# Program order on three engines, and weights halved two dense tiles ahead, in a two-layer decoder step

## Chip, core and metric

The kernel runs on one core of one Trainium2 chip. The metric is the device time of one execution in microseconds (us).

## What is computed

Two layers of a causal decoder for a prompt of 1024 tokens and a group of 8 sample tokens, which together are 1032 columns of a transposed stream `x` (8 blocks of 128 channels).

- Layer 0: RMS norm, one projection into an HGRN2 group and an attention group, an output projection `w_out0`, residual. Then RMS norm and ConvFFN, residual.
- Layer 1: RMS norm, Conformer convolution (GLU from `w_pw1`, depthwise convolution of width 31, LayerNorm over channels, swish, `w_pw2`), residual. Then RMS norm and ConvFFN, residual.
- A final RMS norm.

ConvFFN, with 22 blocks of 128 channels:

```python
g, u = split(h @ w_in)
gc = dwconv3(concat(hist, g))
out = (gelu(gc) * u) @ w_out
```

## The kernel before

**Halved numbers.** Every dense product is made from two parts of each operand: a high part, which ScalarE rounds (`ACT.copy`), and a low part, the difference, which VectorE (or GpSimd) takes. `split` (L102) does it, and `dense2` (L1030) issues three matmuls for each of 8 blocks of the contraction: high by high, high by low, low by high. For weights, `prep` (L106) loads a block of 512 KB into one of two raw buffers (tag `wr`) and `split_halves` (L122) makes two high and two low halves of 128x512. Tags `wh` and `wl` have four buffers each, that is two blocks. Blocks of `w_ffn_out` go through the same two raw buffers, and GpSimd takes their low halves (`oh`, `ol`, six buffers each).

**Tiles.** The columns are worked in two halves: half 0 has 512 columns (24 matmuls a dense tile), half 1 has 520, as two pieces of 260 (48 matmuls). In `mlp` (L1144) `f_in(f)` makes one FFN tile: a dense tile for the gate; ScalarE evacuates it into `gx`, takes the first step of the filter of width 3 and later the GELU; VectorE takes two filter steps; a dense tile for `u`; VectorE's product; the split of that into `ah` and `al`; the output block's load and halves. Behind every second `f_in`, `f_out` makes the output products of the two FFN tiles before (48 matmuls in half 0, 96 in half 1) and VectorE adds them to `x`. Two FFN tiles with one such `f_out` are called a pair here. `f_out_last` (L1228) does the last pair of all, and `finish` (L1389) makes one final tile of 128 tokens: transposes, sum of squares, a reciprocal root by 11 VectorE instructions on one column (`rsqrt_column`), product, store.

**Side work.** Norms and the convolution are generators in the queue `side`. `tick()` (L1119) grants them `rate[0]` units of cost, and each piece yields what it costs. `conv` (L1297) works channel block by channel block: 21 taps on VectorE, accumulated in PSUM (L1318, L1320), and 10 that ScalarE scales (L1304, L1308) and GpSimd adds (L1309); 21 taps with what is beside them cost 15.5 units. `rms_norm` (L1086) and `norm_ln` (L1348) make sums of squares, a mean over channels by a matmul (L1057), and scaled, split outputs. The rates are 2.6, 2.2 in the second projection, and 3.0 in the MLP that carries the second convolution.

**Order of stages from 670 us on:** `w_out0` for half 1; MLP of layer 0, half 0; the same, half 1, five FFN tiles; GLU of half 0 (8 channel blocks), with the first convolution on the side from here; the rest of that MLP; `w_pw2` for half 0; GLU of half 1; MLP of layer 1, half 0, with the second convolution, and within it, after 19 FFN tiles, `w_pw2` for half 1; MLP of layer 1, half 1.

**Order of instructions.** The planner orders each engine's instructions ahead of time, by what it reckons to be ready. From L1415 on TensorE alone is taken out of that and runs in the order of the program:

```python
order.enter_context(tc.manual_schedule(engines={mybir.EngineType.PE}))
```

Of the kernel before, what the change touches and what calls it, by code (L numbers as in the profile page):

```python
# [24 lines left out]
KD = 8  # L25
# [8 lines left out]
def tile_hybrid_step(  # L34
# [76 lines left out]
    class Halves:  # L111


        def __init__(self, pool, tag, bufs):
            self.t = [pool.tile([P, 4, P], F32R, name=tag, tag=tag, bufs=bufs) for _ in range(2)]
# [12 lines left out]
    def wcols(w, c0):  # L128
        return w[:, c0:c0 + P].rearrange("(k p) m -> p k m", p=P)
# [863 lines left out]
    LOW[:] = None, None  # L993
    Y1 = mixed(1)
# [113 lines left out]
    def project(W, h, xt, bias=None):  # L1108
        for m in range(KD):
            w = prep(wcols(W, m * P))  # L1110
            ps = mm2()
            dense2(ps, w, xt, h)
            add_res(m, h, ps, None if bias is None else pv[:, bias + m:bias + m + 1])
            tick()
# [4 lines left out]
    def tick():  # L1119
        side.step(rate[0])  # L1120
# [23 lines left out]
    def mlp(l, h, xt, finish=None):  # L1144
# [14 lines left out]
        def f_in(f):  # L1159
            fc = slice(f * P, (f + 1) * P)  # L1160
            wd = [wfd[:, l, t, f:f + 1] for t in range(3)]
            w = prep(wcols(w_ffn_in[l], f * P))
            ps = mm2()
            dense2(ps, w, xt, h)
# [19 lines left out]
            for t in (1, 2):  # L1184
                DVE.scalar_tensor_tensor(out=ga, in0=gx[:, t:t + m], scalar=wd[t], in1=ga,  # L1185
                                         op0=ALU.mult, op1=ALU.add)
            actf(ga, ga, AF.Gelu)
            tick()
            w = prep(wcols(w_ffn_in[l], NF * P + f * P))
            ps = mm2()  # L1190
            dense2(ps, w, xt, h)
# [8 lines left out]
            wr = wp.tile([P, KD, P], F32, name="wor", tag="wr")  # L1200
            SP.dma_start(wr.rearrange("p k m -> p (k m)"), w_ffn_out[l][fc, :])
            oh, ol = split_halves(wr, fp, "oh", "ol", 6, POOL)
            acts[f] = (ah, al, oh, ol)
            tick()

        def f_out(fs):
            js = [(acts[f][a], acts[f][b]) for f in fs for a, b in ((2, 0), (2, 1), (3, 0))]
            if h == 0:
                for m in range(0, KD, 2):
# [5 lines left out]
                    if m % 4:  # L1215
                        tick()
            else:
                for m in range(KD):
# [6 lines left out]
                    if m % 4 == 3:  # L1225
                        tick()

        def f_out_last(fs):  # L1228

            js = [(acts[f][a], acts[f][b]) for f in fs for a, b in ((2, 0), (2, 1), (3, 0))]  # L1230
            for q in range(2):
# [9 lines left out]
                for t in ((4, 5), (6, 7, 8))[q]:  # L1241
                    for _ in finish(t):
                        pass
# [29 lines left out]
    def glu(k, h, xt):  # L1273
        n = HN[h]
        wa = prep(wcols(w_pw1[0], k * P))
        wg = prep(wcols(w_pw1[0], T + k * P))
        if h == 0:
            pa = pg = mm2()
        else:
            pa, pg = mm2(), mm2()  # L1280
        dense2(pg, wg, xt, h, 1)
        tick()
        dense2(pa, wa, xt, h, 0)
        sg = scratch("ga", 2)[:, :n]
# [214 lines left out]
```

## Time and profile before

| | us |
|---|---|
| median of 3 runs | 2626.59 (2624.08 to 2627.39) |
| the profiled execution | 2624.44 |
| its span, first to last instruction | 2622.7 |

The profile is one execution. Its times are microseconds from the span's start. PE is TensorE's matmuls, PEld its weight loads, DVE VectorE, ACT ScalarE, POOL GpSimd, SP the engine that issues most loads. A row `A <-B` after a bracket or bar says how long the engine was idle before the instruction and what ended that. Matmuls overlap, so the duration of one is more than the spacing of two; the spacing is the stretch divided by the number of them. The mean granted clock of TensorE over the span is 0.981 of full speed.

### The profile page before, as it was taken

Reading aid. Unit: us, or ns where it says so; the run is one execution under the profiler, and the core shown is the slowest. Engines: PE = TensorE matmul, PEld = TensorE weight load, DVE = VectorE, ACT = ScalarE, POOL = GpSimd, SP = SyncE. Lnnn points to the kernel's source line nnn. Section 1 sums busy time; section 2 is a strip of 40 time slices with the busy share of each in tenths; the row PEclk is TensorE's granted clock in tenths of the full one; section 3 lists DMA queues with packets and bytes.
Section 4 is the critical chain, followed back from the end, with each engine's and each line's share of the span. In section 5 each row is a group of like instructions: output and inputs, shape, how many; then the busy total and the mean of one; then the engine's idle time right before and its main releaser. Section 6 shows DMA issues by size and latency. Waiting matters only on the chain.

```text
span 2622.7 us, 40721 instructions
## 1 busy us (share of the span) xinstructions
PE 2484.9 (95%) x15819; PEld 2229.3 (85%) x15819; DVE 1789.2 (68%) x3138; ACT 1229.2 (47%) x2124; POOL 737.1 (28%) x718
## 2 busy tenths in 40 slices
PE   7999998988999999999998999998999998999997
PEld 7888887876978888797998998997777787999997
DVE  7777767776565555479878866859998665654455
ACT  5566645654453333355344455555454542433332
POOL 2111245244211111116354330056663101111110
PEclk9999999999999999999999999999999999999999
DMA  6222244336233333232322322333323322333321
GB/s 200 69 66 65 58 113 141 97 101 187 89 111 98 97 93 100 72 101 81 90 80 74 97 82 65 90 91 97 88 81 97 105 79 79 118 98 90 89 82 57
DMA packets 319908, 247.06 MB, mean 94 GB/s; under 512 B 12055, under 2 KB 292039, under 8 KB 319683
## 3 DMA queue, kind: packets, MB, share of 16 engines
q1 hardware_dynamic: 308899, 213.09, 27.7%
q0 software_dynamic: 10816, 31.38, 4.0%
q8 instruction: 124, 2.03, 0.3%
q14 instruction: 69, 0.57, 0.1%
HBM read 226.82 MB, written 18.73 MB: 94 GB/s over the span
## 4 chain that ended last, share of the span: by engine, by line
PE 36%; DVE 9%; DMA 3%; issue 2%; POOL 2%; ACT 2%; SPq 0%; POOLq 0%; DVEq 0%; ACTq 0%
PE mm L1040 18%; PE mm L1222 9%; PE mm L1037 6%; PE mm L1213 2%; DVE wl L104 2%; DVE dacc L1320 2%; DMA wr<-in_w_ffn_in 2%; DVE ga L1185 1%; DMA wor<-in_w_ffn_out 1%; POOL ol L104 1%; DVE x L1214 1%; ACT wh L103 1%; POOL dp L1309 0%; DVE ga L1195 0%; DVE al L104 0%
## 5 line engine op out<-in xcount | busy, mean ns | idle before, releaser
L103 ACT CAST wh<-wr 128x512 fp32r<-128x512 f32 x536 | 327.0, 617 | 719.7 <-PE mm L1040 280.7
L104 DVE TENSOR_TENSOR wl<-wr,wh 128x512 fp32r<-128x512 f32 x512 | 398.7, 785 | 359.3 <-ACT wh L103 357.5
L1040 PE MATMUL mm<-xn,wh 128*128 128x260 f32 x3840 | 623.2, 285 | 3.1 <-DVE U L1402 2.3
L1037 PE MATMUL mm<-xn,wh 128*128 128x512 f32 x1792 | 558.6, 393 | 2.0 <-ACT wh L103 1.9
L1040 PEld LDWEIGHTS mm<-xn,wh 128*128 128x128 f32 x3840 | 529.9, 189 | 6.3 <-issue 2.9
L104 POOL TENSOR_TENSOR ol<-wor,oh 128x512 fp32r<-128x512 f32 x176 | 245.2, 1412 | 755.0 <-ACT oh L103 408.1
L1037 PEld LDWEIGHTS mm<-xn,wh 128*128 128x128 f32 x1792 | 339.3, 190 | 73.9 <-ACT wh L103 3.1
L1040 PE MATMUL mm<-xn,wl 128*128 128x260 f32 x1920 | 388.3, 284 | 2.6 <-DVE wl L104 2.6
L141 PE MATMUL mm<-xn,wh 128*128 128x260 f32 (+2 forms) x1584 | 385.0, 330 | 0.5 <-ACT qraw L309 0.5
L1037 PE MATMUL mm<-xn,wl 128*128 128x512 f32 x896 | 352.8, 394 | 10.1 <-DVE wl L104 10.0
L1040 PEld LDWEIGHTS mm<-xn,wl 128*128 128x128 f32 x1920 | 297.5, 190 | 2.8 <-DVE wl L104 2.8
L141 PEld LDWEIGHTS mm<-xn,wh 128*128 128x128 f32 x1584 | 267.5, 192 | 27.7 <-issue 8.3
L141 PE MATMUL mm<-xn,wl 128*128 128x260 f32 (+2 forms) x792 | 258.3, 326 | 0.2 <-DVE wl L104 0.2
L1320 DVE SCALAR_TENSOR_TENSOR dacc<-U,wdw,dacc 128x512 f32<-128x512 f32 x304 | 228.1, 750 | 4.7
L1309 POOL TENSOR_TENSOR dp<-dp,s 128x512 f32<-128x512 f32 x144 | 198.7, 1380 | 89.5 <-ACT s L1308 83.7
L1037 PEld LDWEIGHTS mm<-xn,wl 128*128 128x128 f32 x896 | 169.5, 189 | 50.9 <-DVE wl L104 15.3
L1185 DVE SCALAR_TENSOR_TENSOR ga<-gx,wfd,ga 128x544 f32<-128x544 f32 (+1 forms) x176 | 143.0, 813 | 45.6 <-ACT ga L1183 43.4
L1102 DVE TENSOR_TENSOR x<-x,mm 128x520 f32<-128x520 f32 x176 | 121.4, 692 | 63.2 <-PE mm L1222 55.7
L141 PEld LDWEIGHTS mm<-xn,wl 128*128 128x128 f32 x792 | 151.7, 192 | 12.3 <-issue 2.4
L103 ACT CAST oh<-wor 128x512 fp32r<-128x512 f32 x176 | 104.9, 618 | 119.6 <-DMA wor<-in_w_ffn_out 51.7
L1222 PE MATMUL mm<-ah,oh 128*128 128x260 f32 x672 | 140.3, 291 | 19.7 <-DVE ga L1197 10.0
L1213 PE MATMUL mm<-ah,oh 128*128 128x512 f32 x352 | 142.7, 405 | 14.1 <-DVE ga L1195 9.0
(380 smaller groups left out, 4003.4 us busy)
## 6 DMA issues: line engine op xcount, KB each, us to landing
wr<-in_w_ffn_in SPq DMA_DIRECT2D x176, 512.0 KB
wor<-in_w_ffn_out SPq DMA_DIRECT2D x88, 512.0 KB
wr<-in_w_pw SPq DMA_DIRECT2D x48, 512.0 KB
wr<-in_w_in SPq DMA_DIRECT2D x28, 512.0 KB
wr<-in_w_out SPq DMA_DIRECT2D x16, 512.0 KB
xt<-in_x_prompt SPq DMA_DIRECT2D x8, 512.0 KB
xtd<-xs POOLq DMA_DIRECT2D x8, 512.0 KB, 5.2
cb<-cumd SPq DMA_DIRECT2D x8, 512.0 KB
```

The costliest lines, as they stand in the source:

```text
L103: ACT.copy(h, raw)
L104: (eng or DVE).tensor_tensor(out=l, in0=raw, in1=h.bitcast(F32), op=ALU.subtract)
L141: PE.matmul(ps, a[k], b[:, k, :], start=k == order[0] and j == 0, stop=k == order[-1] and j == 2)
L1037: PE.matmul(ps[:, i], a[k], xt[:, r, k], **f)
L1040: PE.matmul(ps[:, q, 0:260], a[k], xt[:, r, k, q * 260:q * 260 + 260], **f)
L1102: DVE.tensor_tensor(out=ways(x[:, m, sl], h), in0=ways(x[:, m, sl], h), in1=outs(ps, h), op=ALU.add)
L1185: DVE.scalar_tensor_tensor(out=ga, in0=gx[:, t:t + m], scalar=wd[t], in1=ga, op0=ALU.mult, op1=ALU.add)
L1213: PE.matmul(ps[:, q], o[m + q], a, start=i == 0, stop=i == len(js) - 1)
L1214: DVE.tensor_tensor(out=x[:, m:m + 2, LO], in0=x[:, m:m + 2, LO], in1=ps, op=ALU.add)
L1222: PE.matmul(ps[:, q, 0:260], o[m], a[:, q * 260:q * 260 + 260], start=i == 0, stop=i == len(js) - 1)
L1309: POOL.tensor_tensor(out=dps[k], in0=dps[k], in1=q, op=ALU.add)
L1320: ins = DVE.scalar_tensor_tensor(out=o, in0=src, scalar=w, in1=accs[k], op0=ALU.mult, op1=ALU.add)
```

## The change

- From L1415 on TensorE, VectorE and ScalarE run in the order of the program; GpSimd and the load queue stay with the planner.
- A table `uses` lists every weight block from the second half of `w_out0` on, in the order of use. `Feed` loads from it through the same two raw buffers and halves dense blocks two dense tiles ahead. Four halves are made before the first tile. After that each dense tile takes one block with `feed.next()`, and two calls of `feed.halve("W")` behind its matmuls make one half each: the first right behind the matmuls, the second behind the evacuation or the residual add. `feed.block()` halves an output block at the end of its FFN tile, with GpSimd taking the low halves as before. A raw buffer's next load is issued when its second half has been made.
- `tick` takes a weight: 0.85 twice in an FFN tile; in `f_out` 0.7 for each of four steps, where it was a whole tick for two.
- The GLU's two tiles take a PSUM tile each, the gate's sigmoid comes before the second tile.
- The projection inside the MLP of layer 1 comes after 18 FFN tiles, not 19.
- In `f_out_last`, final tiles 4 and 5 come behind blocks of the second half, and tiles 6, 7 and 8 after all of them; `finish` takes its reciprocal root for these three from ScalarE's logarithm and exponential and one Newton step of four VectorE instructions.

```diff
+    AT = 18
+
+    def ffn(l, f0=0, f1=NF):
+        for f in range(f0, f1):
+            yield "W", wcols(w_ffn_in[l], f * P)
+            yield "W", wcols(w_ffn_in[l], NF * P + f * P)
+            yield "O", w_ffn_out[l][f * P:(f + 1) * P, :]
+
+    def columns(w):
+        for m in range(KD):
+            yield "W", wcols(w, m * P)
...
+    def glus():
+        for k in range(KD):
+            yield "W", wcols(w_pw1[0], T + k * P)
+            yield "W", wcols(w_pw1[0], k * P)
+
+    uses = [*columns(w_out0[0]), *ffn(0), *ffn(0, 0, 5), *glus(), *ffn(0, 5), *columns(w_pw2[0]),
+            *glus(), *ffn(1, 0, AT), *columns(w_pw2[0]), *ffn(1, AT), *ffn(1)]
+
+    class Feed:
+
+
+        def __init__(self):
+            ws = [u for u in uses if u[0] == "W"]
+            self.seq, n = ws[:2], 2
+            for u in uses:
+                if u[0] == "O":
+                    self.seq.append(u)
+                elif n < len(ws):
+                    self.seq.append(ws[n])
+                    n += 1
+            self.raw, self.q, self.i, self.half, self.cur = {}, [], 0, 0, None
+            self.last = 1 + max(i for i, u in enumerate(self.seq) if u[0] == "W")
+            self.load(0)
+            self.load(1)
+
+        def load(self, i):
+            if i < len(self.seq):
+                kind, ap = self.seq[i]
+                wr = self.raw[i] = wp.tile([P, KD, P], F32, name="wr", tag="wr")
+                SP.dma_start(wr if kind == "W" else wr.rearrange("p k m -> p (k m)"), ap)
+
+        def halve(self, kind):
+
+            if kind == "W" and self.i >= self.last:
+                return
+            assert self.seq[self.i][0] == kind
+            pool, th, tl, bufs = (wp, "wh", "wl", 4) if kind == "W" else (fp, "oh", "ol", 6)
+            if self.half == 0:
+                self.cur = Halves(), Halves()
+                if kind == "W":
+                    self.q.append(self.cur)
+            i = self.half
+            h, l = (pool.tile([P, 4, P], F32R, name=t, tag=t, bufs=bufs) for t in (th, tl))
+            split(self.raw[self.i][:, 4 * i:4 * i + 4], h, l, POOL if kind == "O" else None)
+            self.cur[0].t.append(h)
+            self.cur[1].t.append(l)
+            if i:
+                del self.raw[self.i]
+                self.load(self.i + 2)
+                self.i += 1
+            self.half = 1 - i
+
+        def block(self):
+            self.halve("O")
+            self.halve("O")
+            return self.cur
+
+        def next(self):
+            return self.q.pop(0)
+
+    feed = Feed()
+    for _ in range(4):
+        feed.halve("W")
...
-    def project(W, h, xt, bias=None):
+    def project(h, xt, bias=None):
         for m in range(KD):
-            w = prep(wcols(W, m * P))
             ps = mm2()
-            dense2(ps, w, xt, h)
+            dense2(ps, feed.next(), xt, h)
+            feed.halve("W")
             add_res(m, h, ps, None if bias is None else pv[:, bias + m:bias + m + 1])
+            feed.halve("W")
             tick()
 
     RATE, PROJ, CONV = 2.6, 2.2, 3.0
     rate = [RATE]
 
-    def tick():
-        side.step(rate[0])
+    def tick(w=1.0):
+        side.step(rate[0] * w)
...
             wd = [wfd[:, l, t, f:f + 1] for t in range(3)]
-            w = prep(wcols(w_ffn_in[l], f * P))
             ps = mm2()
-            dense2(ps, w, xt, h)
+            dense2(ps, feed.next(), xt, h)
+            feed.halve("W")
...
                                          op0=ALU.mult, op1=ALU.add)
+            feed.halve("W")
             actf(ga, ga, AF.Gelu)
-            tick()
-            w = prep(wcols(w_ffn_in[l], NF * P + f * P))
+            tick(0.85)
             ps = mm2()
-            dense2(ps, w, xt, h)
+            dense2(ps, feed.next(), xt, h)
+            feed.halve("W")
...
             split(t, ah, al)
-            wr = wp.tile([P, KD, P], F32, name="wor", tag="wr")
-            SP.dma_start(wr.rearrange("p k m -> p (k m)"), w_ffn_out[l][fc, :])
-            oh, ol = split_halves(wr, fp, "oh", "ol", 6, POOL)
+            feed.halve("W")
+            oh, ol = feed.block()
             acts[f] = (ah, al, oh, ol)
-            tick()
+            tick(0.85)
 
...
-                    if m % 4:
-                        tick()
+                    tick(0.7)
...
-                    if m % 4 == 3:
-                        tick()
+                    if m % 2:
+                        tick(0.7)
...
-                for t in ((4, 5), (6, 7, 8))[q]:
-                    for _ in finish(t):
-                        pass
+                    if q and m in (2, 4):
+                        run(finish(3 + m // 2))
+            for t in (6, 7, 8):
+                run(finish(t))
...
-        wa = prep(wcols(w_pw1[0], k * P))
-        wg = prep(wcols(w_pw1[0], T + k * P))
-        if h == 0:
-            pa = pg = mm2()
-        else:
-            pa, pg = mm2(), mm2()
-        dense2(pg, wg, xt, h, 1)
+        pg = mm2()
+        dense2(pg, feed.next(), xt, h)
+        feed.halve("W")
+        sg = scratch("ga", 2)[:, :n]
+        actf(ways(sg, h), outs(pg, h), AF.Sigmoid, bias=pv[:, PV["bpw1"] + 8 + k:PV["bpw1"] + 9 + k])
+        feed.halve("W")
         tick()
-        dense2(pa, wa, xt, h, 0)
-        sg = scratch("ga", 2)[:, :n]
-        actf(ways(sg, h), outs(pg, h, 1), AF.Sigmoid, bias=pv[:, PV["bpw1"] + 8 + k:PV["bpw1"] + 9 + k])
+        pa = mm2()
+        dense2(pa, feed.next(), xt, h)
+        feed.halve("W")
         DVE.scalar_tensor_tensor(out=ways(U[:, k, 30:30 + n], h), in0=outs(pa, h),
                                  scalar=pv[:, PV["bpw1"] + k:PV["bpw1"] + k + 1],
                                  in1=ways(sg, h), op0=ALU.add, op1=ALU.mult)
+        feed.halve("W")
...
+        if t > 5:
+
+            actf(y[:n], ss[:n], AF.Ln, bias=eps_c[:n], scale=1.0 / 1024.0)
+            actf(y[:n], y[:n], AF.Exp, scale=-0.5)
+            DVE.tensor_scalar(out=ss[:n], in0=ss[:n], scalar1=1.0 / 1024.0, scalar2=None,
+                              op0=ALU.mult)
+            newton(y[:n], a[:n], ss[:n], EPS)
...
-    order.enter_context(tc.manual_schedule(engines={mybir.EngineType.PE}))
+    order.enter_context(tc.manual_schedule(engines={mybir.EngineType.PE, mybir.EngineType.Activation,
+                                                  mybir.EngineType.DVE}))
...
-    projected, idle = False, 0
-    for f in range(NF):
-        run(m, 1)
-        idle += not side.q
-        if not projected and (idle == 2 or f == NF - 4):
-            side.drain()
-            project(w_pw2[0], 1, ZB[0], PV["bpw2"])
-            side.add(rms_norm(1, PV["ffn"] + 8, B))
-            projected = True
+    run(m, AT)
+    side.drain()
+    project(1, ZB[0], PV["bpw2"])
+    side.add(rms_norm(1, PV["ffn"] + 8, B))
```

## Rows read from the trace of the kernel before

**Rows 1.** The page, busy time: engine, us, share of the span, instructions.

```profile
PE 2484.9 (95%) x15819; PEld 2229.3 (85%) x15819; DVE 1789.2 (68%) x3138; ACT 1229.2 (47%) x2124; POOL 737.1 (28%) x718
```

**Rows 2.** Busy time by stage: PE, PEld, DVE, ACT, POOL; then PE clock, DMA share, GB/s.

```profile
1094.00:1170.00 76.00, 73.08 (x584) 72.40 (x584) 48.65 (x87) 36.98 (x61) 12.30 (x10) 0.97 0.32 92
...
1170.00:1267.30 97.30, 91.59 (x387) 72.31 (x386) 85.74 (x112) 52.09 (x84) 57.10 (x41) 0.98 0.30 88
...
1267.30:1608.20 340.90, 323.87 (x2616) 321.26 (x2615) 262.96 (x434) 160.24 (x257) 127.41 (x100) 0.97 0.28 81
...
1751.00:2081.70 330.70, 308.48 (x1307) 248.18 (x1308) 294.52 (x376) 175.73 (x296) 172.51 (x140) 0.97 0.31 91
...
2127.80:2203.30 75.50, 70.90 (x294) 56.58 (x292) 47.25 (x63) 29.27 (x48) 11.25 (x9) 0.95 0.26 77
...
2250.40:2587.80 337.40, 337.22 (x2808) 336.96 (x2806) 167.49 (x324) 117.27 (x193) 57.26 (x48) 1.00 0.30 87
...
2587.80:2622.70 34.90, 19.13 (x138) 17.38 (x136) 20.82 (x76) 6.55 (x12) 1.01 (x2) 0.83 0.17 62
```

**Rows 3.** The same columns by pair of FFN tiles, or for several pairs together.

```profile
832.30:1029.70 197.40, 197.40 (x866) 162.29 (x865) 102.26 (x132) 71.79 (x120) 34.45 (x36) 1.00 0.33 96
...
1302.00:1337.00 35.00, 35.00 (x294) 35.00 (x293) 16.13 (x30) 16.15 (x27) 14.21 (x12) 1.00 0.29 86
...
1337.00:1496.80 159.80, 145.51 (x1162) 144.76 (x1161) 143.21 (x227) 70.73 (x117) 80.90 (x61) 0.96 0.28 83
...
1751.00:1789.60 38.60, 35.26 (x146) 28.21 (x147) 32.96 (x40) 25.00 (x42) 28.90 (x24) 0.96 0.37 105
...
1789.60:1970.90 181.30, 170.09 (x722) 136.46 (x721) 175.81 (x226) 90.33 (x155) 111.54 (x90) 0.98 0.29 86
...
1970.90:2005.60 34.70, 33.42 (x146) 26.93 (x145) 27.96 (x37) 12.97 (x24) 9.14 (x8) 1.00 0.36 102
...
2005.60:2048.80 43.20, 36.81 (x154) 29.54 (x153) 31.27 (x41) 24.54 (x41) 17.07 (x14) 0.92 0.29 86
```

**Rows 4.** Timeline of ScalarE, VectorE and TensorE near 1335 us.

```profile
1332.99 1.34 ACT L1308 ACTIVATE s<-U,wdw 128x512 f32<-128x512 f32 x2 [0.65 <-POOL dp L1309]
...
1334.23 0.61 ACT L103 CAST wh<-wr 128x512 fp32r<-128x512 f32 x1
...
1334.87 1.38 DVE L104 TENSOR_TENSOR wl<-wr,wh 128x512 fp32r<-128x512 f32 x1 [6.39 <-ACT wh L103]
...
1346.03 0.77 PE L1222 MATMUL mm<-ah,oh 128*128 128x260 f32 x2 [6.09 <-DVE ga L1197]
```

**Rows 5.** Groups on VectorE, 1770 to 1980 us; the last row 1350 to 1500.

```profile
L1320 DVE SCALAR_TENSOR_TENSOR dacc<-U,wdw,dacc 128x512 f32<-128x512 f32 x121 | 90.7, 750 | 1.8
...
L104 DVE TENSOR_TENSOR wl<-wr,wh 128x512 fp32r<-128x512 f32 x48 | 45.8, 954 | 3.8 <-ACT wh L103 3.7
...
L1185 DVE SCALAR_TENSOR_TENSOR ga<-gx,wfd,ga 128x512 f32<-128x512 f32 x24 | 23.5, 980 | 0.0
...
L104 DVE TENSOR_TENSOR al<-ga,ah 128x512 fp32r<-128x512 f32 x13 | 14.6, 1122 | 0.3 <-ACT ah L103 0.3
...
L1320 DVE SCALAR_TENSOR_TENSOR dacc<-U,wdw,dacc 128x512 f32<-128x512 f32 x73 | 54.7, 749 | 0.8
```

**Rows 6.** Busy time of line 1320 alone in the GLU of half 0.

```profile
1170.00:1267.30 97.30, 46.85 (x63) 0.98 0.30 88
```

**Rows 7.** Timeline of VectorE in the last tile.

```profile
2589.51 0.70 DVE L104 TENSOR_TENSOR al<-ga,ah 128x520 fp32r<-128x520 f32 x1 [0.74 <-ACT ah L103]
```

**Rows 8.** The chain that ended last, near 1372 us: start, us, what.

```profile
1372.17 3.99 DMA wr<-in_w_ffn_in
```

**Rows 9.** Groups on VectorE, 850 to 1000 us.

```profile
L104 DVE TENSOR_TENSOR wl<-wr,wh 128x512 fp32r<-128x512 f32 x36 | 25.0, 706 | 40.2 <-ACT wh L103 40.1
```

**Rows 10.** Line 1094: ns least/median/most, first and last start.

```profile
L1094 DVE SCALAR_TENSOR_TENSOR s<-x,pv,hy x48: 741/749/1798, 687.9 to 2163.0; 128x512 f32<-128x512 f32 x24, 128x520 f32<-128x520 f32 x24
```

**Rows 11.** Timeline of TensorE in the last output blocks.

```profile
2602.07 0.39 PE L1236 MATMUL mm<-ah,oh 128*128 128x260 f32 x1 [1.14 <-DVE x L1239]
```

More of the change, by code (lines that the diff above doesn't have):

```diff
@@ L111, in tile_hybrid_step, with __init__ @@
     class Halves:
-        def __init__(self, pool, tag, bufs):
-            self.t = [pool.tile([P, 4, P], F32R, name=tag, tag=tag, bufs=bufs) for _ in range(2)]
+        def __init__(self, pool=None, tag=None, bufs=0):
+            self.t = [] if pool is None else [pool.tile([P, 4, P], F32R, name=tag, tag=tag, bufs=bufs) for _ in range(2)]
         def __getitem__(self, k):
@@ L1159, in f_in @@
         def f_in(f):
-            fc = slice(f * P, (f + 1) * P)
             wd = [wfd[:, l, t, f:f + 1] for t in range(3)]
-            w = prep(wcols(w_ffn_in[l], f * P))
             ps = mm2()
-            dense2(ps, w, xt, h)
+            dense2(ps, feed.next(), xt, h)
+            feed.halve("W")
             gx = fp.tile([P, 546], F32, name="gx", tag="gx", bufs=2)
@@ L1397, in finish @@
         ACT.activation(row(1)[:n], ps[:n], AF.Square, accum_out=ss[:n])
-        DVE.tensor_scalar(out=ss[:n], in0=ss[:n], scalar1=1.0 / 1024.0, scalar2=EPS,
-                          op0=ALU.mult, op1=ALU.add)
-        rsqrt_column(y[:n], a[:n], ss[:n])
+        if t > 5:
[4 more added lines that the diff above has]
+            newton(y[:n], a[:n], ss[:n], EPS)
+        else:
+            DVE.tensor_scalar(out=ss[:n], in0=ss[:n], scalar1=1.0 / 1024.0, scalar2=EPS,
+                              op0=ALU.mult, op1=ALU.add)
+            rsqrt_column(y[:n], a[:n], ss[:n])
         yo = row(2 + t % 2)
@@ L1414, in tile_hybrid_step @@
     order = ExitStack()
-    order.enter_context(tc.manual_schedule(engines={mybir.EngineType.PE}))
+    order.enter_context(tc.manual_schedule(engines={mybir.EngineType.PE, mybir.EngineType.Activation,
+                                                  mybir.EngineType.DVE}))
     A, B, ZA, ZB = [], [], [], []
     side.add(rms_norm(0, PV["ffn"], A))
-    project(w_out0[0], 1, Y1)
+    project(1, Y1)
     side.drain()
@@ L1434, in tile_hybrid_step @@
     side.add(rms_norm(1, PV["mix"] + 8, B))
-    project(w_pw2[0], 0, ZA[0], PV["bpw2"])
+    project(0, ZA[0], PV["bpw2"])
     side.drain()
```

## Prediction

> **What bounds the kernel now.** I read the busy shares first: TensorE is busy 95% of the span [rows 1], so only its idle time is to be had, and the windows by stage say where that lies [rows 2]. In the plain stretch of the last MLP (2250.4 to 2587.8) TensorE waits for nothing: 2808 records in 337.4 us, 0.120 us each. In a quiet stretch with 512 columns 866 stand in 197.4 us, 0.228 each [rows 3]. These two spacings times a stage's matmuls give what it needs. A pair of FFN tiles with its output blocks has 144 matmuls in half 0, 32.9 us (six pairs in the 197.4), and 288 and a few transposes in half 1, 34.8 (the undisturbed pair from 1302 has 35.0 [rows 3]). The reader is to see in the stages:
> - the GLU of half 0: 384 matmuls, 87.4 us, took 97.3: 10 lost;
> - the MLP of layer 0, half 1, before it: 576 matmuls and some others, 71, took 76.0: 5 lost;
> - the same MLP after the GLU: 2592 and some others, 316, took 340.9: 25 lost;
> - the MLP of layer 1 up to the projection: 1296 and some means, 299, took 330.7: 32 lost;
> - the rest of that MLP: 288, 67, took 75.5: 8 lost;
> - the end: 34.9 us for some 16 us of matmuls and transposes.
>
> The two large losses carry the depthwise convolution, and there VectorE is nearly the bound: in five pairs of half 0 it is busy 175.8 of 181.3 us, in four of half 1 143.2 of 159.8 [rows 3]. The first is a full engine. The second is not: VectorE waits 6.39 us for a weight half, because ScalarE's order has convolution taps ahead of it that are held by GpSimd, and then TensorE stands 6.09 us [rows 4]. So the loss is partly VectorE's amount of work and partly the planner's order.
>
> **Taps in a pair.** A tap takes 0.75 us. In half 0 121 of the common form (19 of every 21) stand in 210 us, 23 in a pair of 36.3; in half 1 73 in 150 us, 21.5 in a pair of 40 [rows 5]. After the change the ticks are 4 x 0.85 + 4 x 0.7 = 6.2 a pair instead of 6; with 15.5 units for 21 taps that is 25.2 taps at 3.0 units (half 0) and 21.8 at 2.6 (half 1).
>
> **The change, part by part** (us, against the profiled execution's 2624.44: a span of 2622.7 and 1.7 around it).
>
> *GLU of half 0.* The planner pulled 63 taps of the common form into it [rows 6]; by the ticks 33 belong there. Per channel VectorE then has 4 weight halves of 0.95, a product of 0.75 and some 7.5 taps, 10.2 against TensorE's 10.9. The loss goes but for a microsecond: **-9**. The other taps move into the next MLP.
>
> *MLP before it.* Little on VectorE, halves ready two tiles ahead: **-4** of the 5.
>
> *Order on VectorE and ScalarE.* This is the cost. Nothing may fill two waits any more. The low half of an activation stands right behind the product that it is made from, with ScalarE's cast between: 0.74 us idle where the trace has it bare [rows 7], twice a pair, 1.5. And a gate block is loaded only when the up block before it has been halved: the load takes 3.99 [rows 8], the cast 0.61 [rows 4]; where no output blocks stand between, only some 3 taps (2.3) cover that: 2.3 once a pair. Behind the waiting cast on ScalarE stand the evacuation of the next tile and its filter's first step, and VectorE's low half with all taps after it; TensorE has two halved tiles in hand, 2 x 5.5 us, so it stops only where VectorE was full already. Of the 3.8 some comes back, since GpSimd runs on while VectorE stands: a low half takes 954 ns in the convolution and 706 in a quiet stretch, the filter steps 980 and the activation's low half 1122 [rows 5, 9]; against 750 and 700 that is 8 x 0.25 + 4 x 0.23 + 2 x 0.42 = 3.7 us of contention a pair, and I take a third, 1.2, as saved. Net 2.6. Bounds: 0.5 (loads covered, the relief kept) and 4.9 (no relief, and 1.1 more where GpSimd, late with an output block, holds the load behind it). I take the middle: both waits have rows, only the relief is a guess.
>
> The VectorE page of the Trainium skill (VectorE: DVE Perf Modes, the TRN2 errata) gives an fp32 tensor_tensor of 512 elements 691 ns, exact; the quiet row agrees, the 954 of the convolution stretch does not. By that figure a pair would have no contention and the sum would be 41 us smaller; the row decides.
>
> *MLP of layer 0 after the GLU.* Busy 35.8 a pair, 0.3 taps more, 2.6 of waits: 39 with small copies. Five pairs carry taps: 195; before they took 35.0 + 159.8 [rows 3]. **0**.
>
> *MLP of layer 1.* Busy 35.2 a pair, 2 taps more (1.5), 2.6 of waits: 39.3; five pairs 196.5 instead of 181.3, +15. The pair ahead of them has 13 taps and is TensorE's again: 33.5 instead of 38.6, -5. The one behind them has 22 taps: 37 instead of 34.7, +2. The norm's first pair took 43.2; with its means in their place 40, -3 [rows 3]. **+9**. The projection after 18 tiles instead of 19 moves 10.9 us of TensorE's work behind it and costs nothing itself.
>
> *Rest of that MLP.* The norm gets four tiles instead of three, but each of its 8 outputs is a product of 0.75 [rows 10], a wait of 0.74 and a low half of 0.7 in order, 17.5 in one pair. **-2** (-4 to +8).
>
> *Seams.* Where a norm ends just ahead of the stage that reads it (first MLP, second GLU), its last outputs come late by the same chain: **+3** (0 to 8).
>
> *Second GLU, first final tiles.* One PSUM tile more a channel and the same work: **-1**.
>
> *The end.* Final tiles 4 and 5 move behind blocks of the second half, which spares TensorE's 1.14 us wait and the like [rows 11]; in three tiles 12 small VectorE instructions become five and two on ScalarE. **-3**.
>
> At nothing: loads, halves and their buffers are as many as before, SP keeps the same 512 KB loads behind the same two buffers. The output blocks' low halves stay on GpSimd, hidden behind more than two tiles of matmuls; with that cover gone the load behind them is late, which is in the upper bound.
>
> Sum: -9 - 4 + 0 + 9 - 2 + 3 - 1 - 3 = -7, 2617.4; the median of the runs lies 2.2 above the profiled execution, so **2620** (own range 2608 to 2632).
>
> **Rivals.**
> - *VectorE's new waits decide (slower).* Place: the 11 pairs with taps. At 4.9 us a pair instead of 2.6 it is 25 more, **2645**; from 3.7 a pair on the kernel is slower by over 0.2%. For it: VectorE has hardly a gap there now, so each wait becomes TensorE's. Against it: GpSimd's interference must then not shrink at all.
> - *GpSimd out of the way (faster).* If loads are covered (0.5 a pair, -23) or half the contention goes (-20): **2597**. For it: halves take 706 in the quiet stretch. Against it: GpSimd has as many taps to add. All contention gone gives 2579; that has 0.03, inside this rival. It is the time that the page's figure asks for.
> - *An order on paper.* If the planner's order was as good where it matters, VectorE's work is conserved and the later pairs give back what the GLU gains: **2627**.
>
> **How the numbers follow.** Forecast 0.38, slower rival 0.28, faster 0.24, no change 0.10. A difference under 0.2% (5.3 us) can't be told from none, so faster means below 2621.3: the faster rival and 0.23 of the forecast, 0.47. Same: 0.12 of the forecast and most of the last rival, 0.21. Slower: the rest, 0.32. The range that leaves out 2 in 10 runs from 2589 to 2648, into both rivals.
>
> **What would show it.** Right: the GLU of half 0 near 88 us; no 6 us wait of VectorE for a weight half; in the pairs with taps a gap of 0.74 before each low half of an activation and one of 2 before a weight half; pairs of about 39. Wrong: pairs of 36 or less, or over 41; new waits at the norms; GpSimd late with output blocks and loads held behind it.

## The result and the profile after

The changed kernel takes 2801.39 us (median of 4 runs) against 2625.34: ratio 1.067, interval 1.065 to 1.070. It is 176 us slower; 2620 was forecast, and even the slower end of the range, 2648, was far off. The profiled execution took 2800.44, its span 2798.7.

The busy times of the page, as in [rows 1]:

```profile
PE 2540.9 (91%) x15819; PEld 2269.9 (81%) x15819; DVE 1742.4 (62%) x3117; ACT 1219.8 (44%) x2129; POOL 703.3 (25%) x718
```

TensorE does as many matmuls as before. VectorE and GpSimd are busy for *less* time than before, and yet everything lasts longer: no engine got more work, the engines wait for each other. TensorE stands idle 257.8 us instead of 137.8, and the same matmuls keep it busy 56 us longer, at a mean granted clock of 0.957 instead of 0.981: 120 and 56 make the 176. The windows by stage (PE, PEld, DVE, ACT, POOL; PE clock, DMA share, GB/s) answer to [rows 2]:

```profile
1121.90:1218.50 96.60, 79.61 (x584) 77.33 (x585) 49.08 (x93) 39.91 (x67) 11.97 (x10) 0.89 0.23 68
1218.50:1306.20 87.70, 87.66 (x387) 71.93 (x386) 52.38 (x75) 43.54 (x71) 30.78 (x23) 1.00 0.37 108
1306.20:1701.20 395.00, 341.55 (x2616) 335.93 (x2615) 282.94 (x470) 163.35 (x266) 144.04 (x119) 0.91 0.24 70
1845.50:2203.00 357.50, 309.78 (x1258) 246.80 (x1258) 278.88 (x382) 168.35 (x285) 157.87 (x138) 0.93 0.26 78
2249.60:2345.90 96.30, 83.52 (x343) 65.47 (x341) 55.84 (x76) 37.62 (x63) 10.89 (x10) 0.95 0.24 71
2397.00:2761.80 364.80, 343.01 (x2807) 339.84 (x2807) 171.29 (x342) 117.56 (x198) 54.00 (x48) 0.99 0.28 83
2761.80:2798.70 36.90, 18.88 (x139) 17.05 (x136) 19.49 (x55) 10.14 (x21) 3.54 (x4) 0.86 0.16 59
```

The GLU of half 0 (second row) is the one stage that gained: 97.3 to 87.7. The row that tells most is the sixth. In the last MLP no taps run, VectorE is busy 171 of 365 us, and still the stage lost 27. Neither VectorE's amount of work nor the convolution can explain that. TensorE's waits in the whole trace (us in total, times, longest):

```profile
PE mm L1297 <- DVE ga L1274: 40.5, 14, 7.1
PE mm L1297 <- DVE x L1178: 36.1, 21, 5.5
PE mm L1289 <- DVE ga L1272: 23.8, 7, 4.5
PE mm L1289 <- DVE x L1290: 18.9, 8, 5.9
```

The same four in the kernel before, where L1222 and L1213 are the output products, made 29.9 us, not 119.3:

```profile
PE mm L1222 <- DVE ga L1197: 10.0, 4, 6.1
PE mm L1213 <- DVE ga L1195: 9.0, 6, 2.1
PE mm L1222 <- DVE x L1102: 7.4, 2, 4.5
PE mm L1213 <- DVE x L1214: 3.5, 2, 2.3
```

All four stand in the output products `f_out`, and what TensorE waits for there is no input of the matmul: the product (L1272, L1274) and the sum into x (L1178, L1290) are the instructions that *read* a PSUM tile and so free it. There are three tiles of two banks (`mm2`, the other two banks serve the convolution and small transposes). A dense tile takes TensorE 5.5 to 5.8 us, so there one tile of lead is ample; an output block takes 1.45 us in half 1, and two of half 0 in one PSUM tile 2.8 us, so there TensorE is ahead of VectorE by two tiles, some 3 and 5.6 us, at most. The timeline of a pair of the last MLP, without taps, shows what VectorE does meanwhile:

```profile
2514.72 1.60 DVE L1261 SCALAR_TENSOR_TENSOR ga<-gx,wfd,ga 128x544 f32<-128x544 f32 x2 [0.97 <-ACT ga L1259]
2514.74 0.40 PE L1297 MATMUL mm<-ah,oh 128*128 128x260 f32 x2
...
2516.24 0.68 DVE L104 TENSOR_TENSOR wl<-wr,wh 128x512 fp32r<-128x512 f32 x1
...
2517.56 0.69 DVE L104 TENSOR_TENSOR wl<-wr,wh 128x512 fp32r<-128x512 f32 x1 [0.63 <-ACT wh L103]
2518.17 0.69 DVE L1272 TENSOR_TENSOR ga<-ga,mm 128x520 f32<-128x520 f32 x1
2518.89 0.16 DVE L1274 TENSOR_TENSOR ga<-ga,mm 128x8 f32<-128x8 f32 x1
2519.14 0.63 ACT L103 CAST ah<-ga 128x520 fp32r<-128x520 f32 x1 [1.61 <-DVE ga L1274]
...
2519.20 0.48 PE L1297 MATMUL mm<-ah,oh 128*128 128x260 f32 x2 [1.40 <-DVE ga L1274]
```

The up product ends at 2514.7. VectorE multiplies it into the gate only at 2518.17, behind a low half of a weight (2516.24) and another one that waits for its cast (2517.56). Those halves are for dense tiles that start at 2529.1 and 5.8 us later. The product frees TensorE's third block, which stands 1.40 us. VectorE's order is not all of it. The product also needs the GELU, which ends only at 2517.02: on ScalarE the copy of the gate (2512.63) stands behind a cast whose weights have just landed, though the gate's matmuls ended at 2508.9. The chain that ended last between 2500 and 2520 shows that load and that cast:

```profile
2508.11 3.91 DMA wr<-in_w_ffn_in
2512.10 0.63 ACT wh L103
```

So the two orders act together here: ScalarE's brings the gate late, and VectorE's half at 2517.56 adds the last 1.1 us. With taps in the same place it is worse:

```profile
1469.48 0.62 ACT L103 CAST wh<-wr 128x512 fp32r<-128x512 f32 x1 [3.04 <-DMA wr<-in_w_ffn_in]
...
1470.13 0.69 DVE L104 TENSOR_TENSOR wl<-wr,wh 128x512 fp32r<-128x512 f32 x1 [3.08 <-ACT wh L103]
...
1473.43 0.41 PE L1297 MATMUL mm<-ah,ol 128*128 128x260 f32 x2
1473.62 0.68 DVE L104 TENSOR_TENSOR wl<-wr,wh 128x512 fp32r<-128x512 f32 x1
...
1474.22 3.12 DVE L1396 SCALAR_TENSOR_TENSOR dacc<-U,wdw,dacc 128x512 f32<-128x512 f32 x4
...
1477.25 1.06 DVE L104 TENSOR_TENSOR wl<-wr,wh 128x512 fp32r<-128x512 f32 x1
1478.24 0.68 DVE L1272 TENSOR_TENSOR ga<-ga,mm 128x520 f32<-128x520 f32 x1
...
1479.27 0.77 PE L1297 MATMUL mm<-ah,oh 128*128 128x260 f32 x2 [3.98 <-DVE ga L1274]
```

The late load (3.04) shifts the filter, four taps and another weight half follow, and TensorE stands 3.98 us. Two matmuls then take 0.77 us where they took 0.41 (1473.43): the granted clock was 1.00 from 1473 to 1475 and is 0.50 from 1479.3 to 1482, behind the stop. The last kind of loss is at the norms:

```profile
2120.69 0.62 ACT L103 CAST wh<-wr 128x512 fp32r<-128x512 f32 x1 [3.80 <-DMA wr<-in_w_ffn_in]
...
2121.09 0.60 PE L1133 MATMUL mean<-hy,mean_d 128*128 128x260 f32 x2
...
2129.38 0.37 ACT L1134 COPY hy<-mean 128x260 f32<-128x260 f32 x1
...
2129.80 1.23 PE L1133 MATMUL mean<-hy,mean_d 128*128 128x260 f32 x2 [8.11 <-ACT hy L1134]
```

The mean's first part is done at 2121.7, but the copy that frees its bank stands in ScalarE's order behind the casts of a whole tile, one of which waits 3.80 us for a load. TensorE's next matmul waits 8.11 us.

**Theory**, from here on: a strict order on VectorE puts what nobody needs soon (halves, taps, norm steps) ahead of what frees PSUM. **Rivals**: the table with its two raw buffers makes weights or blocks late; ScalarE's order is the cause; VectorE is simply full.

### The profile page after: what moved, and what is told of

Same layout as the page of the kernel before. It is cut to its first block, busy times and chain, and to the rows that moved or that the text cites. A ratio compares the mean times of both kernels' runs of the same rounds, so it can differ in the third digit from the quotient of the medians.

```text
span 2798.7 us, 40518 instructions
## 1 busy us (share of the span) xinstructions
PE 2540.9 (91%) x15819; PEld 2269.9 (81%) x15819; DVE 1742.4 (62%) x3117; ACT 1219.8 (44%) x2129; POOL 703.3 (25%) x718
## 4 chain that ended last, share of the span: by engine, by line
PE 55%; DVE 20%; ACT 7%; issue 6%; DMA 6%; POOL 2%; SPq 0%; ACTq 0%; DVEq 0%; POOLq 0%
PE mm L1116 16%; PE mm L1113 14%; PE mm L141 8%; PE mm L1297 6%; PE mm L1289 5%; DVE wl L104 5%; DMA wr<-in_w_ffn_in 4%; DVE dacc L1396 4%; DVE ga L1261 2%; ACT wh L103 1%; DVE al L104 1%; DVE ga L1272 1%; ACT ah L103 1%; DVE x L1290 1%; ACT ga L1259 1%
## 5 line engine op out<-in xcount | busy, mean ns | idle before, releaser
L104 DVE TENSOR_TENSOR wl<-wr,wh 128x512 fp32r<-128x512 f32 x512 | 371.4, 726 | 412.2 <-ACT wh L103 401.2
L1116 PEld LDWEIGHTS mm<-xn,wh 128*128 128x128 f32 x3840 | 532.6, 190 | 10.9 <-ACT wh L103 3.7
L104 POOL TENSOR_TENSOR ol<-wr,oh 128x512 fp32r<-128x512 f32 x176 | 230.0, 1327 | 646.8 <-ACT oh L103 613.4
L1297 PE MATMUL mm<-ah,oh 128*128 128x260 f32 x672 | 151.2, 309 | 87.7 <-DVE ga L1274 40.5
L1385 POOL TENSOR_TENSOR dp<-dp,s 128x512 f32<-128x512 f32 x144 | 187.5, 1302 | 129.1 <-ACT s L1384 122.7
L1289 PE MATMUL mm<-ah,oh 128*128 128x512 f32 x352 | 150.0, 426 | 47.1 <-DVE ga L1272 23.8
L1297 PEld LDWEIGHTS mm<-ah,oh 128*128 128x128 f32 x672 | 114.3, 208 | 96.3 <-issue 42.8
L1261 DVE SCALAR_TENSOR_TENSOR ga<-gx,wfd,ga 128x544 f32<-128x544 f32 (+1 forms) x176 | 135.2, 768 | 69.1 <-ACT ga L1259 66.0
L1178 DVE TENSOR_TENSOR x<-x,mm 128x520 f32<-128x520 f32 x176 | 117.8, 692 | 56.7 <-PE mm L1297 53.1
```

The lines of the kernel that those rows point to most:

```text
L104: (eng or DVE).tensor_tensor(out=l, in0=raw, in1=h.bitcast(F32), op=ALU.subtract)
L1116: PE.matmul(ps[:, q, 0:260], a[k], xt[:, r, k, q * 260:q * 260 + 260], **f)
L1178: DVE.tensor_tensor(out=ways(x[:, m, sl], h), in0=ways(x[:, m, sl], h), in1=outs(ps, h), op=ALU.add)
L1289: PE.matmul(ps[:, q], o[m + q], a, start=i == 0, stop=i == len(js) - 1)
L1297: PE.matmul(ps[:, q, 0:260], o[m], a[:, q * 260:q * 260 + 260], start=i == 0, stop=i == len(js) - 1)
L1385: POOL.tensor_tensor(out=dps[k], in0=dps[k], in1=q, op=ALU.add)
```

## The experiments

All times are those of single runs beside the kernel before on the same chip (2626.9 to 2630.6 us) unless said otherwise. Executions of the kernel before range from 2617.5 to 2631.4, so a step of some 15 us rests on the stages that it changes, in the table of experiment 6, more than on its total.

**1. Which engine's order.** The changed kernel with fewer engines held in order:

```diff
-    order.enter_context(tc.manual_schedule(engines={PE, Activation, DVE}))
+    order.enter_context(tc.manual_schedule(engines={PE}))              # e1
+    order.enter_context(tc.manual_schedule(engines={PE, Activation}))  # e2
+    order.enter_context(tc.manual_schedule(engines={PE, DVE}))         # e3
```

> The changed kernel with only TensorE held to program order; the planner orders VectorE and ScalarE again, everything else of the change (halving two dense tiles ahead, one table of blocks, GLU in two products, the end) stays. Order theory (strict order on VectorE puts halves and side work ahead of the evacuations that free TensorE's three PSUM tiles): nearly all of the 176 us come back, 2605 to 2650 us, GLU of half 0 near 88 us. Feed theory (halving from the table through two raw buffers makes blocks or weights late): stays at 2740 to 2800 us.

> The changed kernel with TensorE and ScalarE held to program order and VectorE left to the planner. Order theory, which puts the loss on VectorE: 2610 to 2690 us, under half of the loss. ScalarE theory (casts ahead of the copy and Gelu, ping-pong between the two engines): 2720 to 2800 us. Feed theory: 2740 to 2800 us.

> The changed kernel with TensorE and VectorE held to program order and ScalarE left to the planner. Order theory: most of the loss is here, 2730 to 2800 us. ScalarE theory: 2610 to 2690 us. Feed theory: 2740 to 2800 us.

Measured: 2654.35, 2682.19 and 2786.29 us. VectorE's order costs 132 us by itself, ScalarE's 28, the two together 147. The table with its buffers is in all of them, so by itself it isn't the bulk. But 2654 is 4 above what the theory allowed: the change without any new order is still 26 us slower than the kernel before.

By stage the two orders divide differently. From the end of its first `f_out` on, the plain stretch of the last MLP took 325.9 us before and 344.6 after, but 325.9 in e2 and 326.9 in e3: without taps either order alone costs next to nothing there, and the loss needs both. Where taps run, VectorE's order alone is enough: MLP 0's half 1 behind the GLU took 405.7 in e3 and 351.5 in e2, against 367.3 in e1 and 394.9 in the changed kernel.

**2. Is it the evacuations?** In x7 the product moves ahead of the weight half that stood between it and the up tile's matmuls; in x1 the copy of the gate moves ahead of a half too.

```diff
             dense2(ps, feed.next(), xt, h)
-            feed.halve("W")                 # x1 only
             gx = fp.tile([P, 546], F32, name="gx", tag="gx", bufs=2)
...
+            feed.halve("W")                 # x1 only: behind the copies into gx
             ga = scratch("ga", 2)[:, :m]
...
             dense2(ps, feed.next(), xt, h)
-            feed.halve("W")
...
             DVE.tensor_tensor(out=ways(t, h), in0=ways(t, h), in1=outs(ps, h), op=ALU.mult)
...
+            feed.halve("W")
             split(t, ah, al)
```

> Only one half of the first move: the product of the two halves stands ahead of the weight halves; the copy of the gate's product stays behind them. If the product is what frees the PSUM tile too late, nearly all of the 86 us of the whole move: 2715 to 2740 us, plain stretch 337 to 346 us. If the gate's chain (copy, filter, Gelu) behind the first half is what makes the product late: 2770 to 2800 us.

> Only the first of the two moves of the run before: evacuations ahead of the weight halves, side work where the change put it. Order theory: the plain stretch of the last MLP (364.8 us, before 337.4) comes down to some 345 to 352, because there nothing but the halves stands ahead of the product; the stretches with taps lose little, since their taps still stand ahead of the sums into x; 2765 to 2785 us in all. If the taps ahead of the sums were harmless, this alone would give the 2739 us of both moves.

Measured: x7 2739.83, x1 2715.72. One instruction's place, the product's, is worth 62 us, at the edge of what was expected, and the gate's copy 24 more. By stage 18 of the 62 stand in the last MLP and 32 in the two MLPs with taps; 7 stand in the start, which x7 does not touch. I had expected only 16 to 36 from x1: these moves help in the stretches with taps too, not only in the plain one. In the plain stretch x7 leaves one wait of TensorE (2373 to 2700 us):

```profile
PE mm L1297 <- DVE x L1178: 0.4, 1, 0.4
```

**3. Is it PSUM?** The order of the change is kept, and the last MLP's half 1 gets a fourth tile.

```diff
+    def extra(name):
+        return bank.tile([P, 2, 512], F32, name=name, tag="ex")
...
     def one(tag, name):
-        return bank.tile([P, 512], F32, name=name, tag=tag)
+        if tag == "misc" and not plain:
+            return mm2()[:, 0]
+        return extra(name)[:, 0]
...
-                    ps = mm2()
+                    ps = extra("mm2") if plain and m % 4 == 3 else mm2()
...
+    plain.append(1)                 # ahead of the last MLP's half 1
```

> The changed kernel with its order as it is, and a fourth PSUM tile for the output products of the last MLP's half 1: the two banks of the accumulator of the convolution and of the small transposes serve as one more tile there, where no convolution runs (elsewhere the small transposes take one of the three tiles). PSUM theory: TensorE can be one block of 1.45 us further ahead, so that the plain stretch of the last MLP falls from 364.8 us to 344 to 354, pairs from 36.9 to 35.0 to 35.8. Theory that VectorE's order delays something other than PSUM (weights, activations): 360 to 367 us there.

Measured: 2786.17 in all and 354.5 in the plain stretch, just above the range. From the end of its first `f_out` on, that stretch took 325.8 before, 344.6 after, 334.6 with the fourth tile and 325.4 in x1. TensorE's waits there, first in the changed kernel (2417 to 2762 us):

```profile
PE mm L1297 <- DVE x L1178: 7.9, 9, 1.2
PE mm L1297 <- DVE ga L1274: 7.4, 6, 1.5
```

and with the fourth tile (2413 to 2748 us):

```profile
PE mm L1304 <- DVE ga L1281: 7.8, 5, 2.4
```

The waits for the sums are gone: block 3, counted from 0, has a tile of its own. The waits for the product stay, since block 2 still takes the up product's tile. So half of the loss there goes by adding PSUM alone, at an unchanged order, and all but a microsecond of it by moving the product (326.8 in x7): in this stretch PSUM's release is the way by which the order reaches TensorE. Where taps run, no tile was added; there the rows point the same way (in MLP 0's half 1 behind the GLU 26.1 us of TensorE's waits for the product and 23.1 for the sums), and so does what x7 gave back. The Trainium skill says of such a pattern that the same gap repeating on the engine that should be saturated can mean that there isn't enough SBUF or PSUM for the next tile to be allocated (Perfetto Trace Analysis, Optimization Strategy). These runs agree as to PSUM, and add that here the cheaper remedy is to release earlier.

**4. Where the side work stands.** On top of x1, x3 puts all side work from the even tile to the last sum behind that sum; x4 spreads it.

```diff
             acts[f] = (ah, al, oh, ol)
-            tick(0.85)
+            if f % 2 or not f:
+                tick(0.85)
...
-                        tick(0.7)      # between the sums
+                        tick(0.5)      # x4 only
+            tick(3.65)                 # x3; x4: tick(1.65), behind the last sum
```

> The changed kernel with two moves in the program order and nothing else: in an FFN tile the copy of the gate's product and the product of the two halves stand ahead of the weight halves, and the side work that stood between an even tile's product and the eight sums into x, or between the sums, is issued behind the last sum in one lump. Order theory: TensorE's waits for VectorE inside the output products nearly vanish (pairs with taps from 42 to 45 us to 37 to 40, plain pairs from 36.9 to 35), 2640 to 2700 us. Feed theory: no part of this touches the loads, 2780 to 2810 us. Theory that VectorE is simply full there: the work is the same, 2770 to 2800 us.

> Both moves, but the side work is not one lump of 3.65 ticks behind the sums: half a tick stands behind every second sum (1.5 us of taps into the 1.5 us that two sums leave free) and 1.65 ticks behind the last. Order theory in its second form (a lump of 10.5 us of taps makes the next tile's product late, and breaks the spacing of the norm's steps): pairs with taps from 41 to 42 us to 38 to 40, the last two pairs of the first MLP's half 1 from 105 us to 85 to 95, 2690 to 2725 us. Theory that VectorE is full in those pairs: no change, 2730 to 2745 us.

Measured: x3 2738.97, worse than x1 with its one move and outside every range that I had set, and x4 2692.86, inside its range. The lump is seen in x3's timeline of VectorE:

```profile
1463.66 4.71 DVE L1395 SCALAR_TENSOR_TENSOR dacc<-U,wdw,dacc 128x512 f32<-128x512 f32 x6
1468.47 0.75 DVE L1395 SCALAR_TENSOR_TENSOR s<-U,wdw,dacc 128x512 f32<-128x512 f32 x1
1469.25 0.76 DVE L1393 TENSOR_SCALAR dacc<-U,wdw 128x512 f32<-128x512 f32 x1
1470.04 3.92 DVE L1395 SCALAR_TENSOR_TENSOR dacc<-U,wdw,dacc 128x512 f32<-128x512 f32 x5
```

Ten microseconds of taps in one piece make the next copy, filter and product late; dosed into the time that two sums leave free, the same taps do not. That falls against "VectorE is full": the work is the same, and MLP 0's half 1 behind the GLU went from 391.1 (x3) to 353.2 (x4).

**5. The norms.** On top of x4, x5 issues each mean later; y1 also takes the RMS norm's outputs in pairs; y2 counts a pair at its cost.

```diff
-    WAIT = 2.0
+    WAIT = 4.0          # x5, y1, y2
...
-        for k in range(KD):
+        for k in range(0, KD, 2):    # y1, y2: two products, then two casts and low halves
...
-            yield 1.2
+            yield 2.4                # y2: 4.0
```

> The run with both moves and paced side work (2693 us) with one number changed: the spacing that a norm leaves ahead of each mean is 4.0 units of side work for 2.0. Theory of the means: in that run TensorE waited some 26 us in all ahead of a mean whose squares were still being summed (gaps of 5.2, 5.6, 4.9, 4.2, 6.4 us); with the mean issued later most of these go, 2665 to 2680 us. Theory that the chain between ScalarE, VectorE and GpSimd is what lasts so long, wherever the mean stands: the waits move to the tiles behind, 2685 to 2700 us.

> The 2677 us run with the RMS norm's output steps in pairs: two products, two casts, two low halves, so that VectorE doesn't stop for ScalarE's cast between a product and its low half (47.9 us of such waits at 60 steps in the changed kernel). Theory that these waits delay the first pairs behind each norm: 2655 to 2670 us. Theory that the norm's steps are paced too fast, with or without waits: 2672 to 2682 us.

> The same, with a pair of output steps counted at 4.0 units of side work for 2.4 (its four VectorE instructions take 2 x 0.97 + 2 x 0.7 us). Pace theory: the first output products behind a norm (gaps of 4 to 9 us) come near their 11.7 us, 8 to 15 us below the run with pairs alone. Theory of the waits: within 4 us of it.

Measured: 2677.45, 2651.38 and 2665.52. The later means gave 15 us, the pairs 26 more, beyond what I had expected; the true count lost 14 where one theory had a gain and the other no change, so neither holds as it was put; it mended the first MLP's half 0 (384.0 to 377.1) and lost most in layer 1's half 0 (469.8 to 480.4). How long VectorE stood ahead of the low halves `xn` of the norms (us, times), in x5:

```profile
  ACT xn L103: 48.4, 59
```

and in y1:

```profile
  ACT xn L103: 15.5, 11
```

**6. The rest.** e5 is e1 with the evacuations of x1, e6 is e1 with the side work in the places of the kernel before. e4 is the kernel before with the three engines in order and without halving ahead. b1 is the kernel before with the change's GLU alone:

```diff
...
-        if h == 0:
-            pa = pg = mm2()
-        else:
-            pa, pg = mm2(), mm2()
-        dense2(pg, wg, xt, h, 1)
+        pg = mm2()
+        dense2(pg, wg, xt, h)
+        sg = scratch("ga", 2)[:, :n]
+        actf(ways(sg, h), outs(pg, h), AF.Sigmoid, ...)
         tick()
-        dense2(pa, wa, xt, h, 0)
...
+        pa = mm2()
+        dense2(pa, wa, xt, h)
```

> VectorE and ScalarE left to the planner as in the first run (2654 us), with the evacuations written ahead of the weight halves. If the 26 us by which that run is over the kernel before come from halves that the planner ranks by the order in which they are written, ahead of the product: 2615 to 2635 us. If they come from the table's loads (two raw buffers, blocks late): 2648 to 2660 us.

> The first run (planner for VectorE and ScalarE, 2654 us) with the side work at the places and in the amounts of the kernel before. If its 26 us over the kernel before come from the new places of the side work: 2615 to 2632 us. If they come from the halving two tiles ahead: 2645 to 2660 us.

> The kernel before, with ScalarE and VectorE in program order too and nothing else of the change: weights are prepared right ahead of the dense tile that reads them. If the halving two tiles ahead is what makes a strict order possible at all, TensorE waits for a cast and a low half at each of some 200 dense tiles, 4 to 6 us each: 3300 to 3900 us. If the strict order costs the same with or without it: 2780 to 2850 us.

> The kernel before with one part of the change alone: the GLU of half 0 uses two PSUM tiles and takes the gate's product first, its sigmoid running beside the second product. If GLU's gain is that and needs no program order: GLU of half 0 from 97.5 to 87 to 91 us, half 1 93 to 97, in all 2612 to 2622 us. If the gain came from the weights' earlier halving or the strict order: 97 us, 2624 to 2630 us.

Measured: e5 2651.91 and e6 2653.05, so neither the writing order nor the new places of the side work explains the 26 us of e1. They stand in MLP 0's half 1 behind the GLU, 367.3 for 340.9, where y1, with all three engines in order, took 341.6; what the planner makes of the halving ahead stays open. e4 took 4031.33, more than expected. There the waits are for weights, which the changed kernel hardly shows:

```profile
PE mm L1037 <- ACT wh L103: 398.6, 87, 11.9
PE mm L1040 <- ACT wh L103: 372.8, 80, 9.0
```

The halving ahead does its part: without it a strict order costs 1400 us, with it 176. b1 took 2620.27 against 2626.85 (medians of 11 and 15 executions), ratio 0.998, interval 0.997 to 0.999: 0.2% faster than the kernel before. Its GLU of half 0:

```profile
1169.70:1258.70 89.00, 88.60 (x387) 71.69 (x387) 81.22 (x108) 50.39 (x82) 56.09 (x39) 1.00 0.32 93
```

The group of its taps in that stretch:

```profile
L1318 DVE SCALAR_TENSOR_TENSOR dacc<-U,wdw,dacc 128x512 f32<-128x512 f32 x57 | 42.8, 752 | 1.2
```

The stages side by side, in us from the first matmul of each to the first of the next (MLP 0 and 1 are the layers; the first row ends behind the first projection; up to that projection, ahead of what the change orders, the traces took 669 to 678 us, 670.1 before and 677.8 after, and why was not followed):

| stage | before | after | x7 | x1 | x4 | x5 | y1 | e1 |
|---|---|---|---|---|---|---|---|---|
| start, first projection | 717.1 | 726.3 | 719.0 | 719.3 | 724.4 | 721.6 | 718.5 | 715.9 |
| MLP 0, half 0 | 376.8 | 395.6 | 394.5 | 393.1 | 389.1 | 391.1 | 384.0 | 376.5 |
| half 1 to the GLU | 76.1 | 96.6 | 95.3 | 92.9 | 86.8 | 81.5 | 79.8 | 79.5 |
| GLU, half 0 | 97.3 | 87.7 | 87.1 | 87.1 | 87.1 | 87.5 | 87.1 | 91.0 |
| MLP 0, half 1, rest | 340.9 | 394.9 | 373.6 | 363.4 | 353.2 | 342.0 | 341.6 | 367.3 |
| projection, GLU of half 1 | 142.9 | 144.4 | 142.9 | 142.8 | 142.8 | 149.6 | 142.2 | 140.1 |
| MLP 1, half 0, projection | 456.8 | 505.1 | 494.6 | 488.4 | 481.0 | 474.5 | 469.8 | 458.0 |
| MLP 1, half 1 | 379.8 | 411.2 | 392.8 | 388.3 | 388.4 | 389.4 | 388.4 | 390.2 |
| end | 35.0 | 36.9 | 38.2 | 38.3 | 38.4 | 38.3 | 38.3 | 34.1 |

So of the 176 us the corrections of experiments 2, 4 and 5 took back 62 + 24 + 23 + 15 + 26 = 150 with the order kept on all three engines; some 6 of these, and 8 of the 176, lie in the start ahead of the first projection. What is left (2651 to about 2628) stands where norms or final tiles run beside an MLP's first pairs and at the end; it was not followed further.

## Why the prediction was wrong, point by point

**The step that failed** is one sentence, "TensorE has two halved tiles in hand, 2 x 5.5 us, so it stops only where VectorE was full already." It took the halved weights for the limit of TensorE's lead. The weights did lie ready; the limit in the output products is the three PSUM tiles, that is some 3 us in half 1 and 5.6 in half 0, and VectorE need not be full for that, only late once. Experiments 2 and 3 show it for the plain stretch, where by experiment 1 it takes both orders to make VectorE late; where taps run, the waits and what the moves gave back speak for it. From that sentence followed that a stage without taps could lose nothing, and so the last MLP's pairs do not stand in the sum at all: that MLP lost 31 us, 27 of them in the plain stretch, where VectorE was busy 171 of 365 us.

**VectorE's own account** was nearly right in half 0, and not in half 1. Its groups in MLP 1 (1845 to 2060, 11 tiles' worth), as in [rows 5]:

```profile
L104 DVE TENSOR_TENSOR wl<-wr,wh 128x512 fp32r<-128x512 f32 x45 | 38.0, 844 | 17.5 <-ACT wh L103 17.5
L1261 DVE SCALAR_TENSOR_TENSOR ga<-gx,wfd,ga 128x512 f32<-128x512 f32 x22 | 16.5, 750 | 3.7 <-ACT ga L1259 3.3
L104 DVE TENSOR_TENSOR al<-ga,ah 128x512 fp32r<-128x512 f32 x11 | 7.6, 692 | 7.5 <-ACT ah L103 7.5
```

Per pair (5.5 of them) the wait ahead of a weight half is 3.2 and ahead of the low half of an activation 1.4, with 0.6 before the filter: 5.2 for the 3.8 forecast. The relief is 8 x 0.11 + 4 x 0.23 + 2 x 0.43 = 2.7 for the 1.2 forecast, so the net is 2.5 for 2.6. The five pairs with taps took 202.4 us for the 196.5 forecast. The faster rival was right that VectorE's instructions get shorter, and that still gave no time. In the five pairs of MLP 0's half 1 (1341.8 to 1559.8) VectorE waited for ScalarE 9.0 a pair, 45.0 in all, over twice the 3.8:

```profile
DVE wl L104 <- ACT wh L103: 17.6, 12, 3.1
DVE ga L1261 <- ACT ga L1259: 10.7, 11, 1.0
DVE glast L1252 <- ACT gx L1250: 9.2, 5, 2.3
DVE al L104 <- ACT ah L103: 7.5, 10, 0.8
```

Two of these rows, the filter and the small copies behind the gate's copy, had no term in the sum. Three sums of the prediction don't come out of its own terms: with 1.2 of the 3.7 of contention already taken as saved, all of it gone is 27 us more and not 41, half of it 7 and not 20, and the lower bound of a pair is 0.3 and not 0.5. None of this moves the forecast.

**MLP 1, half 0**: forecast +9, measured to the end of its eighth `f_out` +37. The five pairs are 6 over; the first pair was right (32.8). The pair with the 8.11 us wait for the mean's copy took 49.8 for the 37 forecast, the eighth `f_out` 19.2 for 11.2. **MLP 0, half 1**: forecast 0, measured +54: the five pairs with taps 218 for 195, and 30 behind them, where the layer norm runs. In the five pairs VectorE was busy 168.8 of 218: the slower rival had the place, but not the mechanism, and its 2645 took VectorE's waits one to one, at 4.9 a pair.

**The small terms**: half 1 before the GLU -4, measured +20.5 (its first `f_out` 29.3 us); seams +3, measured +19 in the first MLP's half 0 alone; the rest of MLP 1's half 0 -2, measured 96.3 for 75.5 with one tile of 10.9 more in it, +10; the end -3, measured +2. All were costed by VectorE's work, with no PSUM tile and no ScalarE copy behind the waits.

**The GLU of half 0**: -9, measured -9.6, and it is the one large term that came out, but for another reason than given. The sum took it from the taps that the planner had pulled in. b1 leaves 57 of the 63 taps there [rows 6], has VectorE busy 81.2 of 89.0 us, and gains 8.3 all the same. What counts is what b1 changes: gate and value have a PSUM tile each, and the sigmoid runs beside the value's matmuls instead of behind both; the two were not tried apart. The sum puts "One PSUM tile more a channel" at the second GLU; by the diff that one, half 1, had two tiles already, and the new one is in half 0.

Of the named signs the 0.74 gap came as forecast (0.72 in the mean, 63.2 us at 88 low halves), and the gap of 2 before a weight half was 3 a pair, and the longest wait for one in the pairs with taps was 4.3; "new waits at the norms" and pairs over 41 stood on the list of what would make it wrong, and both came.

## What to carry to other kernels

When an engine is put into program order, ask of each instruction on it not only how long it takes but which buffer it frees, and how far the producer can run without that buffer: that lead is the smallest of all its resources, here 3 us of PSUM in half 1 against 11 us of weights. Judge the orders of several engines together: in the plain stretch each alone was harmless. Write evacuations first, work for later tiles behind them, and dose filler work into the gaps instead of in lumps. Preparing weights ahead makes a strict order possible; it doesn't by itself make it good.

## What was not expected of the hardware

- Stops cost more than their length. In MLP 0's half 1 behind the GLU the same 2616 matmuls kept TensorE busy 341.55 us instead of 323.87, beside 36 us more of standing, at a mean granted clock of 0.91 instead of 0.97; after the 3.98 us wait above, at a granted clock of 0.50, two matmuls took 0.77 us instead of 0.41, which is the level of 1.2 GHz for that of 2.4.
- VectorE's instructions in the convolution stretch of MLP 1, which the prediction took to be slowed by GpSimd, got shorter with the same taps on GpSimd: low halves of activations from 1122 to 692 ns, filter steps from 980 to 750, weight halves from 954 to 844, where the quiet stretch has 706. Whether it is overlap with GpSimd that went, and which, was not tested.
